# Tiles 10 to 13 of the second down projection as seven block products, and a reordered last norm

## The chip, the cores and the metric

The kernel runs on one core of one Trainium2 chip. The metric is the device time of one execution in microseconds (us), lower is better. A core has TensorE (PE, matmuls; PEld is its loading of the stationary operand), VectorE (DVE), ScalarE (ACT), GpSimd (POOL) and SyncE (SP, which here only issues DMAs). Each works through its own queue in order and waits for the others by semaphores. SBUF is the on-chip memory, PSUM holds the matmuls' sums in banks.

## The reference

A decoder trunk of two layers over 512 positions of 1024 channels. Each layer has a mixer and a gated feed-forward part (FFN) with a convolution of width 3 along the positions; a last RMS norm ends it. The change lies in layer 1's FFN and in the last norm:

```python
def gated_conv_ffn(x, w_gate, w_up, conv_w, conv_b, w_down):
    g = jnp.einsum('bsd,df->bsf', x, w_gate)
    g = causal_dwconv3(g, conv_w) + conv_b
    up = jnp.einsum('bsd,df->bsf', x, w_up)
    return jnp.einsum('bsf,fd->bsd', jax.nn.silu(g) * up, w_down)

hn = rms_norm(h, norm_ffn[layer])
h = h + gated_conv_ffn(hn, ...)
...
return rms_norm(h, final_norm)
```

All is float32. `D_FF` is 2816, that is 22 tiles of 128 hidden rows; the kernel calls such a tile `ft`, 0 to 21.

## The kernel before, in words

**Three matmuls for one.** A float32 operand is split into a high part, rounded to the type that TensorE takes at full rate (`F32R`), and a low part, the rest. Each product of two operands is three matmuls: high by high, high by low, low by high. ACT writes the high part (a copy). The low part is made in one of two ways. `parts` has DVE subtract the high part from the source. `summed` has ACT write the source with the sign turned into the low part's tile, and a DMA issued by POOL then accumulates the source onto it. That DMA waits for ACT's copy, and the tile may be used when it has landed.

**The steps of the FFN.** `Ffn.hidden(f)` makes the hidden tiles f and f+1 (f = 0, 2, ... 20; "step f"). From f = 2 on, gate (g) and up (u) are each multiplied by Strassen's scheme: seven block products in place of eight, so 14 per step, each of 12 matmuls of 128x256. The order is written out in `products`: g1, u1, g5, g6, u5, u6, g2, g7, u2, u7, g4, g3, u4, u3 (letter and number of the product). The weights and their sums (`s12`, `s34`) are made by `prepare(f)` on DVE and split into high and low parts. g's products 1, 6, 7 and 4 use one PSUM bank one after the other (`BANK`, "a"): ACT copies the bank to SBUF (`after`, L736), and only then may PE start the next product in it. DVE adds the other products onto these copies (L741, L746), then come the scaling by the norm's factor (L756), the convolution (L576), the silu on ACT (L584), and the multiplication with the up rows (L760 to L766). The results are the rows `s`, one 128x512 tile for each ft.

**The down projection of layer 1.** `split_acts` splits rows into high and low parts (L260, L262). `half_down(a, b, half)` multiplies the tiles a to b-1 with half of the 1024 output columns: for four tiles 4 x 4 x 3 = 48 matmuls of 128x512. DVE adds the four sums onto `y[t]` (L1104), t being one of four tiles of 128 positions. `STEPS` says which half follows which step: after step 6 the tiles 2 to 5 with half 0, after step 8 with half 1, and so on. So tiles 10 to 13 come after step 14 (half 0) and after step 16 (half 1), tiles 14 to 17 after 18 and 20.

**The last four tiles, 18 to 21.** They are multiplied by Strassen's scheme as well: the rows and the positions make a 2 by 2 block matrix, and so do the weights, `raw_dn18_00` to `_11` with four fetches. Seven products of 12 matmuls of 128x512 replace two halves of 48. `less` makes four sums of weights on DVE, the rows' sums are made on half rows of 128x256, `block` splits them into `hg` tiles (which are free then), and `put` splits the weights with `summed`. `product(p, i)` issues six matmuls for one block row i, `add` brings the sum into y. A product's sum goes to two places in Strassen's scheme; here it is folded into the operands so that each product's sum is added once per block row, 14 adds in all.

**The tail.** While those seven run, the last norm of each finished row begins. `taken` is an add into y, `squared` an ACT pass that sums squares, `halved` a 128x1 step on DVE, `rooted` ACT's square root, `inverted` three 128x1 steps on DVE, `times` the product of a row with the norm's gain, and `scaled` the multiplication with the row's factor, with the DMA that writes it out. `inorder` keeps the order in which these lines are written.

**What sets the order.** Outside the tail, a scheduler orders each engine's queue when the program is built. `behind(ins, first)` sets only an order, and in the down part `less` is placed behind `ffn.added["u"]`, the DVE add after u's product 7. Tiles share buffers by tag: four buffers for raw weights (`raw`), six each for high and low parts (`whi`, `wlo`), four each for the rows' high and low parts (`ahi`, `alo`), three for sums of weights (`sum`). A fetch into a raw buffer waits until the last reader of its former tile is done.

Of the kernel before, what the change touches and what calls it, by code (L numbers as in the profile page):

```python
# [15 lines left out]
P = 128  # L16
D = 1024
# [14 lines left out]
def tile_trunk(ctx: ExitStack, tc: tile.TileContext, x, norm_mix, norm_ffn, final_norm,  # L32
# [13 lines left out]
    def mm_bank(name):  # L46
        return ps_mm.tile([P, 512], F32, tag="mm", name=name)
# [505 lines left out]
    class Ffn:  # L553
# [10 lines left out]
        def __init__(self, layer, prm, norm, ap, sums):  # L564
            self.layer, self.prm, self.ap, self.acts = layer, prm, ap, {}
            self.norm, self.sums = norm, sums
# [13 lines left out]
        def silu(self, c, ft):  # L580
            name = f"s{self.layer}_{ft}"
            s = (self.ap.tile([P, S], F32, tag="s", bufs=3, name=name) if ft % 2 else
                 tp.tile([P, S], F32, tag="sq", name=name))
            nc.scalar.activation(s, c, AF.Silu, bias=self.prm("bf", ft))  # L584
            return s
# [493 lines left out]
    def ffn1(norm):  # L1079
        with tc.tile_pool(name="f1", bufs=1) as ap:  # L1080
# [4 lines left out]
            ffn = Ffn(1, prm1, norm, ap, sums)  # L1085
# [21 lines left out]
            def half_down(a, b, half):  # L1107
# [13 lines left out]

            a = NF - 4
            rows = {ft: row for ft, row in ffn.steps(half_down, before)}
            raw = {(i, j): fetch(
                w_ffn_down[1][(a + 2 * i) * P : (a + 2 * i + 2) * P, j * 512 : j * 512 + 512]
                .rearrange("(k p) c -> p k c", p=P), 2, 512, f"dn{a}_{i}{j}")
                for i, j in ((0, 0), (0, 1), (1, 1), (1, 0))}
            fin = ap.tile([P, D], F32, tag="sum", bufs=3, name="fin")  # L1130
            nc.scalar.dma_start(
                fin, final_norm.rearrange("(o d) -> o d", o=1).to_broadcast([P, D]))
            b11, b12, b21, b22 = (raw[at][0] for at in ((0, 0), (0, 1), (1, 0), (1, 1)))
            t1, t2 = (ap.tile([P, 2, S], F32, tag="sum", bufs=3, name=f"dnt{i}") for i in (1, 2))
            stat = {}

            def put(product, how, src):
                stat[product] = how(src, 2, 512, f"dnp{product}")

            def less(dst, x, y_):  # L1140
                behind(nc.vector.tensor_tensor(dst, x, y_, ALU.subtract), ffn.added["u"])

            less(t1, b12, b11)
            put(1, summed, b11)
            put(2, summed, b21)
            less(t2, b22, t1)
            put(5, summed, t1)
            put(6, summed, t2)
            less(b12, b22, b12)
            put(3, summed, b22)  # L1150
            put(7, summed, b12)
            less(b21, b21, t2)
            put(4, summed, b21)

            blocks = {}

            def block(product, n, srcs):
                hi, lo = (x.rearrange("p (a b) -> p a b", a=2) for x in hg[n])
                blocks[product] = hi, lo
                if not isinstance(srcs, list):  # L1160
                    nc.scalar.activation(hi, srcs, AF.Copy)
                    nc.vector.tensor_tensor(lo, srcs, hi.bitcast(F32), ALU.subtract)
                    return None
                for i, src in enumerate(srcs):
                    ins = nc.scalar.activation(hi[:, i], src, AF.Copy)
                    nc.vector.tensor_tensor(lo[:, i], src, hi[:, i].bitcast(F32), ALU.subtract)
                return ins

            a11, a12 = ([rows[a + 2 * i + n][:, :HALF] for n in range(2)] for i in range(2))
            a21, a22 = ([rows[a + 2 * i + n][:, HALF:] for n in range(2)] for i in range(2))  # L1170
            s1, s2 = (ap.tile([P, 2, HALF], F32, tag="c", bufs=2, name=f"dns{i}") for i in (1, 2))
            block(1, 0, a11)
            block(2, 1, a12)
            for n in range(2):
                nc.vector.tensor_tensor(s1[:, n], a21[n], a22[n], ALU.add)
            block(5, 4, s1)
            for n in range(2):
                nc.vector.tensor_tensor(s2[:, n], s1[:, n], a11[n], ALU.subtract)
            block(6, 5, s2)
            for n in range(2):  # L1180
                nc.vector.tensor_tensor(a12[n], a12[n], s2[:, n], ALU.subtract)
            last_split = block(3, 6, a12)
            for n in range(2):
                nc.vector.tensor_tensor(a21[n], a11[n], a21[n], ALU.subtract)
            block(7, 2, a21)
            block(4, 3, a22)
# [3 lines left out]
            banks = {}  # L1190

            def product(p, i, c0=0, c1=512, bank=None):

                at = bank or BANK[p], i
                first = at not in banks
                if first:
                    banks[at] = mm_bank(f"dn{a}_{at[0]}{i}")
                ps = banks[at][:, c0:c1]
                cs = slice(i * P, (i + 1) * P)
                (l_hi, l_lo), (r_hi, r_lo) = blocks[p], stat[p]  # L1200
                for k in range(2):
                    for l, r, end in ((l_hi, r_hi, False), (l_hi, r_lo, False),
                                      (l_lo, r_hi, k == 1)):
                        nc.tensor.matmul(ps, l[:, k, cs], r[:, k, c0:c1], start=first, stop=end,
                                         skip_group_check=True)
                        first = False
                return ps
# [5 lines left out]
            def taken(p, i, cs, bank=None):  # L1213

                t = i + 2 * (p in (5, 7, 4))
                part = cs if bank else slice(0, 512)
                inorder(add(y[t][:, cs], product(p, i, part.start, part.stop, bank), t))
# [6 lines left out]
            def halved(t, cs, first):  # L1224

                ss, ms = ssf[:, t, cs.start // 256 : cs.start // 256 + 1], ssf[:, t, 3:4]
                inorder(vec.tensor_scalar(ms, ss, -0.5 / D, -0.5 * EPS, op0=ALU.mult, op1=ALU.add)
                        if first else
                        vec.scalar_tensor_tensor(ms, ss, -0.5 / D, ms, op0=ALU.mult, op1=ALU.add))
# [4 lines left out]
            def inverted(t):  # L1234
                ms, r = ssf[:, t, 3:4], factor[t]
                inorder(vec.reciprocal(r, root[t]))
                inorder(vec.scalar_tensor_tensor(ms, ms, r, r, op0=ALU.mult, op1=ALU.mult))
                inorder(vec.scalar_tensor_tensor(r, ms, 1.5, r, op0=ALU.add, op1=ALU.mult))
# [35 lines left out]
            times(vec, 2, left)  # L1274
# [13 lines left out]
            squared(1, right)  # L1288
            halved(3, left, False)
            rooted(3)  # L1290

            first, second = slice(0, 256), slice(256, 512)
            taken(2, 1, first, "c")
            squared(1, first)
            halved(1, right, True)
            taken(2, 1, second, "d")
# [48 lines left out]
```

## Time and profile before

| | |
|---|---|
| time, median of 3 runs | 988.8 us (988.59 to 989.36) |
| the profiled execution | 988.85 us, its span 987.1 us |
| DVE busy | 775.9 us, 79% of the span |
| ACT busy | 562.0 us, 57% |
| POOL busy | 112.0 us, 11% |
| granted TensorE clock, mean | 0.998 |
| HBM | 102 GB/s over the span |

The span is what the profiler sees of the engines' work; the time holds 1.75 us more. In rows of the timeline the columns are the start and the length of an instruction in us, its engine, its line in the kernel, the operation, output <- inputs, and the shape; a bracket gives the idle time before it and what ended it. Matmuls are pipelined, so that the length of one (0.39 us) is more than the distance between two starts. A DVE or ACT row also is somewhat longer than the distance to the next start. Buffer numbers are left out of names: `raw_dn` stands for each weight tile of the down part. SPq and POOLq are the DMAs that these queues issue, with the time from the issue to the landing as the last number of a row in the view of issues.

### The profile page before, as it was taken

To read this page: it belongs to the slowest core of one execution; us is meant where nothing else is said; L and a number is where in the kernel's file an instruction comes from. 1 tells how busy PE (TensorE), PEld (TensorE's weight loads), DVE (VectorE), ACT (ScalarE), POOL (GpSimd) and SP (SyncE) were. 2 spreads that over 40 slices of the span, in tenths; PEclk is the share of its full clock that TensorE was granted. 3 is DMA by queue.
4 is the path that set the end of the run, shared out by engine and by line. 5 is a ranking of instruction groups with operands and counts; after the bars stand their busy time and mean duration, and the time that the engine had idled before them with its cause. 6 is when DMAs were issued, how large, how long until landed. Compare 5 with 4: busy or idle time off the path is not lost.

```text
span 987.1 us, 15485 instructions
## 1 busy us (share of the span) xinstructions
PE 975.2 (99%) x6099; PEld 879.9 (89%) x6099; DVE 775.9 (79%) x1181; ACT 562.0 (57%) x843; POOL 112.0 (11%) x129
## 2 busy tenths in 40 slices
PE   9999999999999999999999999999999999999996
PEld 6788888999999999999889988889999999999985
DVE  5797458998788887886887765589987779777787
ACT  5623347755465654655488734576655456554675
POOL 2142022000000000000210001210000000000022
PEclk9999999999999999999999999999999999999999
DMA  7442225555465454653324623264565465445573
GB/s 248 131 150 85 86 86 128 135 137 157 129 150 133 132 142 129 150 130 108 126 64 120 198 69 106 55 140 128 150 166 133 130 149 147 119 135 135 161 151 116
DMA packets 87942, 129.32 MB, mean 131 GB/s; under 512 B 4309, under 2 KB 57789, under 8 KB 87869
## 3 DMA queue, kind: packets, MB, share of 16 engines
q1 hardware_dynamic: 78172, 98.69, 32.2%
q0 software_dynamic: 8208, 27.79, 15.5%
q10 hardware_dynamic: 1488, 1.84, 0.6%
q8 instruction: 48, 0.79, 0.3%
q14 instruction: 26, 0.20, 0.1%
HBM read 98.42 MB, written 2.10 MB: 102 GB/s over the span
## 4 chain that ended last, share of the span: by engine, by line
PE 85%; DVE 8%; ACT 2%; issue 1%; DMA 0%; POOL 0%; ACTq 0%; DVEq 0%
PE dn L153 3%; PE dn L154 3%; PE dn L155 3%; PE d L153 3%; PE d L154 3%; PE d L155 3%; PE oo L155 1%; PE oo L153 1%; PE oo L154 1%; PE oe L154 1%; PE oe L153 1%; PE oe L155 1%; PE u_20a L542 1%; PE u_18a L542 1%; PE u_16a L542 1%
## 5 line engine op out<-in xcount | busy, mean ns | idle before, releaser
L576 DVE SCALAR_TENSOR_TENSOR c<-rows,prm,c 128x512 f32<-128x512 f32 x88 | 64.1, 747 | 1.5 <-ACT c L574 1.4
L140 POOL DMA_DIRECT2D wlo_g<-raw_g x20 | 17.2, 859 | 387.4 <-ACT wlo_g L139 350.4
L153 PE MATMUL d<-a_hi,whi_d 128*128 128x512 f32 x144 | 56.1, 390 | 0.0
L153 PE MATMUL dn<-whi_dn,a_hi 128*128 128x512 f32 x144 | 56.1, 390 | 0.0
L154 PE MATMUL dn<-wlo_dn,a_hi 128*128 128x512 f32 x144 | 56.1, 390 | 0.0
L154 PE MATMUL d<-a_lo,whi_d 128*128 128x512 f32 x144 | 56.1, 390 | 0.0
L155 PE MATMUL d<-a_hi,wlo_d 128*128 128x512 f32 x144 | 56.0, 389 | 0.0
L155 PE MATMUL dn<-whi_dn,a_lo 128*128 128x512 f32 x144 | 56.0, 389 | 0.0
L679 DVE TENSOR_TENSOR wlo_s34u<-s34u,whi_s34u 128x1024 fp32r<-128x1024 f32 x20 | 24.5, 1224 | 25.5 <-ACT whi_s34u L678 25.5
L149 DVE TENSOR_TENSOR wlo_dn<-raw_dn,whi_dn 128x1024 fp32r<-128x1024 f32 x18 | 22.0, 1225 | 23.6 <-ACT whi_dn L148 23.4
L142 ACT ACTIVATE whi_u<-raw_u 128x1024 fp32r<-128x1024 f32 x21 | 22.2, 1055 | 31.6 <-PE d L154 17.5
L149 DVE TENSOR_TENSOR wlo_d<-raw_d,whi_d 128x1024 fp32r<-128x1024 f32 x18 | 22.0, 1224 | 19.5 <-ACT whi_d L148 19.5
L198 ACT ACTIVATE hgh<-h,prm 128x512 fp32r<-128x512 f32 x24 | 17.3, 722 | 35.1 <-DVE h L309 35.0
L140 POOL DMA_DIRECT2D wlo_u<-raw_u x21 | 18.1, 860 | 162.0 <-ACT wlo_u L139 83.7
L584 ACT ACTIVATE s<-c,prm 128x512 f32<-128x512 f32 x44 | 31.2, 714 | 7.3 <-DVE c L576 7.2
L209 POOL TENSOR_TENSOR ssq_f<-ssq_f,sq_f 128x512 f32<-128x512 f32 x14 | 19.7, 1410 | 132.3 <-ACT sq_f L208 97.5
L260 ACT ACTIVATE a_hi<-s 128x512 fp32r<-128x512 f32 x40 | 25.0, 626 | 15.7 <-PE dn L154 9.9
L199 DVE SCALAR_TENSOR_TENSOR hgl<-h,prm,hgh 128x512 fp32r<-128x512 f32 x24 | 23.2, 965 | 12.0 <-ACT hgh L198 11.9
L155 PEld LDWEIGHTS d<-a_hi,wlo_d 128*128 128x128 f32 x144 | 27.0, 188 | 5.7
L155 PEld LDWEIGHTS dn<-whi_dn,a_lo 128*128 128x128 f32 x144 | 27.0, 188 | 5.7
L1104 DVE SCALAR_TENSOR_TENSOR y<-dn,small,y 128x512 f32<-128x512 f32 x40 | 27.7, 748 | 5.5 <-PE dn L155 5.5
L153 PEld LDWEIGHTS d<-a_hi,whi_d 128*128 128x128 f32 x144 | 27.1, 188 | 5.3
(1489 smaller groups left out, 3762.7 us busy)
## 6 DMA issues: line engine op xcount, KB each, us to landing
raw_g<-in_w_ffn_gate_dram SPq DMA_DIRECT2D x40, 512.0 KB, 3.8
raw_u<-in_w_ffn_up_dram SPq DMA_DIRECT2D x40, 512.0 KB, 3.7
raw_dn<-in_w_ffn_down_dram SPq DMA_DIRECT2D x22, 512.0 KB, 3.6
wlo_u<-raw_u POOLq DMA_DIRECT2D x21, 512.0 KB, 5.7
wlo_g<-raw_g POOLq DMA_DIRECT2D x20, 512.0 KB, 4.6
raw_d<-in_w_ffn_down_dram SPq DMA_DIRECT2D x18, 512.0 KB, 3.7
raw_oe<-in_w_out_even_dram SPq DMA_DIRECT2D x8, 512.0 KB, 3.6
raw_v<-in_w_in_odd_dram SPq DMA_DIRECT2D x8, 512.0 KB, 4.5
```

The lines of the kernel that those rows point to most:

```text
L140: nc.gpsimd.dma_start(lo, raw, accum_op=ALU.add)
L149: behind(nc.vector.tensor_tensor(lo, raw, hi.bitcast(F32), ALU.subtract), after[0])
L153: nc.tensor.matmul(ps, lhs[0], rhs[0], start=start, stop=False)
L154: nc.tensor.matmul(ps, lhs[0], rhs[1], start=False, stop=False)
L155: nc.tensor.matmul(ps, lhs[1], rhs[0], start=False, stop=stop)
L199: nc.vector.scalar_tensor_tensor(hg[k][1], h[k], g, hg[k][0].bitcast(F32), op0=ALU.mult, op1=ALU.subtract)
L260: nc.scalar.activation(hi, src, AF.Copy, scale=scale)
L542: nc.tensor.matmul(ps, l, r, start=first, stop=end, skip_group_check=True)
L576: nc.vector.scalar_tensor_tensor(c, t[:, i : S + i], prm("cf", i * NF + ft), c, op0=ALU.mult, op1=ALU.add)
L584: nc.scalar.activation(s, c, AF.Silu, bias=self.prm("bf", ft))
L679: nc.vector.tensor_tensor(lo, src, hi.bitcast(F32), ALU.subtract)
L1104: return nc.vector.scalar_tensor_tensor(dst, ps, ffn.cols[:, t : t + 1], dst, op0=ALU.mult, op1=ALU.add)
```

## The change

The code of the last four tiles becomes a class `Seven`, which can be used for any four tiles, and it is used for tiles 10 to 13 too (`sevens = (10,)`). The main loop of layer 1's FFN is written out in `ffn1` instead of in `steps`. After step 12 `part.acts` splits the rows of tiles 10 to 13 and makes their sums; the rows stay whole for that, and the silu of tile 14 writes into a tile with the tag `ssq`. After step 14 `part.weights` fetches and splits the weights (products 3, 7 and 4 by DVE, the other four with accumulating DMAs), and `part.run` issues the seven products. After step 16 no down part follows. In the tail, 128x1 steps on DVE become `tensor_scalar` with the second operand as a scalar per partition, three of the products with the gain move from DVE to GpSimd, two scalings move to DVE and two of row 1's squares become one.

```diff
+            if ft in self.apart:
+                s = tp.tile([P, S], F32, tag="ssq", bufs=1, name=name)
...
+            class Seven:
...
+                def block(self, product, srcs, home=None):
+                    name = f"dnb{self.a}_{product}"
+                    hi, lo = home or (ap.tile([P, S], F32R, tag=f"a{x}", bufs=4,
+                                              name=f"{name}_{x}") for x in ("hi", "lo"))
...
+                def acts(self, rows, home={}):
+                    a = self.a
+                    a11, a12 = ([rows[a + 2 * i + n][:, :HALF] for n in range(2)]
+                                for i in range(2))
+                    a21, a22 = ([rows[a + 2 * i + n][:, HALF:] for n in range(2)]
+                                for i in range(2))
+                    s1, s2 = (ap.tile([P, 2, HALF], F32, tag="c", bufs=2, name=f"dns{a}_{i}")
+                              for i in (1, 2))
+                    self.block(1, a11, home.get(1))
+                    self.block(2, a12, home.get(2))
+                    for n in range(2):
+                        nc.vector.tensor_tensor(s1[:, n], a21[n], a22[n], ALU.add)
+                    self.block(5, s1, home.get(5))
...
+                def weights(self, between, by_vector=()):
...
+                    def put(product, src):
+                        how = parts if product in by_vector else summed
+                        self.stat[product] = how(src, 2, 512, f"dnp{a}_{product}")
+
+                    def less(dst, x, y_):
+                        behind(nc.vector.tensor_tensor(dst, x, y_, ALU.subtract),
+                               ffn.added["u"])
+
+                    less(t1, b12, b11)
+                    put(1, b11)
+                    put(2, b21)
+                    less(t2, b22, t1)
+                    put(5, t1)
+                    put(6, t2)
+                    less(b12, b22, b12)
+                    put(3, b22)
+                    put(7, b12)
+                    less(b21, b21, t2)
+                    put(4, b21)
...
+                def run(self):
+                    for p in (1, 2, 5, 6, 3, 7, 4):
+                        for i in range(2):
+                            t = i + 2 * (p in (5, 7, 4))
+                            cs = left if p in (1, 2, 4) else right
+                            add(y[t][:, cs], self.product(p, i), t)
+                        if p in (1, 2, 5):
+                            self.block(*self.rest.pop(0))
...
+            part = None
+            for f in range(0, NF, 2):
+                multiplied(f)
+                a = f - 4
+                if part:
+                    part.weights(lambda: None, (3, 7, 4))
+                    part.run()
...
+                    split_rows(f + 1, f)
...
+                if f > 0 and f % 4 == 0 and f - 2 in sevens:
+                    part = Seven(f - 2)
+                    part.acts(rows)
...
-                inorder(vec.tensor_scalar(ms, ss, -0.5 / D, -0.5 * EPS, op0=ALU.mult, op1=ALU.add)
-                        if first else
-                        vec.scalar_tensor_tensor(ms, ss, -0.5 / D, ms, op0=ALU.mult, op1=ALU.add))
+                inorder(vec.tensor_scalar(ms, ss, -0.5 / D, -0.5 * EPS if first else ms,
+                                          op0=ALU.mult, op1=ALU.add))
...
-                inorder(vec.scalar_tensor_tensor(ms, ms, r, r, op0=ALU.mult, op1=ALU.mult))
-                inorder(vec.scalar_tensor_tensor(r, ms, 1.5, r, op0=ALU.add, op1=ALU.mult))
+                inorder(vec.tensor_scalar(ms, ms, r, r, op0=ALU.mult, op1=ALU.mult))
+                inorder(vec.tensor_scalar(r, ms, 1.5, r, op0=ALU.add, op1=ALU.mult))
...
-            times(vec, 2, left)
+            times(pool, 2, left)
...
+            times(pool, 3, right)
...
-            scaled(act, 2, left)
-            scaled(pool, 2, right)
+            scaled(act, 2, right)
...
-            times(vec, 3, right)
+            scaled(vec, 2, left)
...
-            squared(1, right)
+            times(pool, 1, right)
...
+            scaled(vec, 3, left)
+            scaled(pool, 3, right)
```

In the built order of the changed kernel, PE has 12 matmuls fewer, DVE 24 instructions more, ACT 13 and POOL 4 more. DVE makes the sums of step 16's weights behind the last add of the seven, and PE starts the first four matmuls with the high parts of step 16 within the seven.

More of the change, by code (lines that the diff above doesn't have):

```diff
@@ L553, in tile_trunk, with __init__ @@
     class Ffn:
-        def __init__(self, layer, prm, norm, ap, sums):
+        def __init__(self, layer, prm, norm, ap, sums, apart=()):
             self.layer, self.prm, self.ap, self.acts = layer, prm, ap, {}
+            self.apart = apart
             self.norm, self.sums = norm, sums
@@ L1083, in sums @@
                         for k in (kp, kp + NP)]
-            ffn = Ffn(1, prm1, norm, ap, sums)
+            sevens = (10,)
+            ffn = Ffn(1, prm1, norm, ap, sums, [a + 4 for a in sevens])
             acts = ffn.acts
@@ L1120, in half_down @@
                       lambda t, ps: add(y[t][:, cs], ps, t))
[L1124 to L1129, printed above, removed]
-            fin = ap.tile([P, D], F32, tag="sum", bufs=3, name="fin")
@@ L1131, in ffn1 @@
[L1131 to L1178, printed above, removed]
@@ L1188, in ffn1, with fetch_fin @@
+            last = Seven(NF - 4)
+            fin = ap.tile([P, D], F32, tag="sum", bufs=3, name="fin")
+            def fetch_fin():
+                nc.scalar.dma_start(
+                    fin, final_norm.rearrange("(o d) -> o d", o=1).to_broadcast([P, D]))
+            last.weights(fetch_fin)
+            homes = dict(zip((1, 2, 7, 4, 5, 6, 3), hg))
+            last.acts(rows, homes)
+            last_split = [last.block(*x) for x in last.rest][0]
             first_root = work("sd", 1, "first")
@@ L1189, in ffn1 @@
             behind(nc.scalar.activation(first_root, eps, AF.Sqrt), last_split)
[L1190 to L1207, printed above, removed]
@@ L1216, in taken @@
                 part = cs if bank else slice(0, 512)
-                inorder(add(y[t][:, cs], product(p, i, part.start, part.stop, bank), t))
+                inorder(add(y[t][:, cs], last.product(p, i, part.start, part.stop, bank), t))
             def squared(t, cs):
```

100 lines of the change are left out of this document (79 added, 21 removed).

## The prediction

> **What bounds the kernel now.** First the totals and the chain of waits on the page of before, then the stages one by one.
>
> ```profile
> PE 975.2 (99%) x6099; PEld 879.9 (89%) x6099; DVE 775.9 (79%) x1181; ACT 562.0 (57%) x843; POOL 112.0 (11%) x129
> PE 85%; DVE 8%; ACT 2%; issue 1%; DMA 0%; POOL 0%; ACTq 0%; DVEq 0%
> ```
>
> TensorE (PE) sets the end nearly everywhere. So a removed matmul shortens the run, as long as the other engines still deliver in time. Whether they do is a question of the stretch that changes. The view of busy time by stretch gives, for step 14 with its down half, step 16 with its down half, and that down half alone:
>
> ```profile
> 833.98:865.04 31.06, 31.06 (x217) 29.16 (x216) 24.22 (x37) 16.43 (x24) 1.72 (x2) 1.00 0.53 141
> 865.04:896.10 31.06, 31.06 (x217) 29.17 (x216) 24.68 (x39) 17.63 (x27) 1.72 (x2) 1.00 0.51 132
> 854.13:865.04 10.91, 10.91 (x50) 9.02 (x49) 9.22 (x15) 5.58 (x7) 1.72 (x2) 1.00 0.74 190
> ```
>
> The columns are the length, then busy time of PE, its weight loads, VectorE (DVE), ScalarE (ACT), GpSimd (POOL), the granted clock (1.00), DMA share and GB/s. PE has no gap. DVE is busy 24.22 + 24.68 = 48.9 us of 62.1, which leaves 13.2 us over two steps. Step 14 holds 14 products before its down half, 20.15 / 14 = 1.44 us each.
>
> **The saving on PE.** Two down halves for tiles 10 to 13 go (2 x 48 matmuls of 128x512) and seven products of 12 such matmuls come. The last seven of before show what one product costs:
>
> ```profile
> 958.22 0.39 PE L1204 MATMUL dn_a<-whi_dnp,hgh 128*128 128x512 f32 x1
> 960.94 0.39 PE L1204 MATMUL dn_b<-whi_dnp,hgh 128*128 128x512 f32 x1
> ```
>
> Twelve matmuls lie between these starts: 2.72 us. Seven are 19.04 us against 2 x 10.91 = 21.82. The gain is 2.75 us, the middle between that difference and 12 matmuls at 2.72 / 12.
>
> **The price on DVE.** The spacing of starts, not the busy time, counts for a queue that never rests:
>
> ```profile
> 856.69 0.42 DVE L760 TENSOR_TENSOR s<-kept,s 128x256 f32<-128x256 f32 x1
> 857.02 0.42 DVE L761 TENSOR_TENSOR s<-u_14a,s 128x256 f32<-128x256 f32 x1
> 857.36 1.22 DVE L679 TENSOR_TENSOR wlo_s12g<-s12g,whi_s12g 128x1024 fp32r<-128x1024 f32 x1
> 858.49 0.69 DVE L766 TENSOR_TENSOR s<-kept,s 128x512 f32<-128x512 f32 x1
> 859.09 1.22 DVE L679 TENSOR_TENSOR wlo_s34g<-s34g,whi_s34g 128x1024 fp32r<-128x1024 f32 x1
> ...
> 863.20 2.79 DVE L1104 SCALAR_TENSOR_TENSOR y<-dn,small,y 128x512 f32<-128x512 f32 x4 [1.69 <-PE dn L155]
> ```
>
> That is 0.335 for 128x256, 1.13 for 128x1024, 0.60 for 128x512 and about 0.66 for an add into y (2.79 for four). Added: 4 `less` (4.52), 3 low parts of weights (3.39), 8 sums of half rows (2.68), low parts of row blocks (10 x 0.335 + 2 x 0.60 = 4.55), 14 adds into y (9.24): 24.4 us. Removed: 4 low parts of weights (4.52), 4 of rows (2.40), 8 adds (5.28): 12.2 us. The net 12.2 us would nearly fill the 13.2, while the two steps shrink by 2.75. It fits only if evenly spread, and it isn't: `less` of t1 is ordered behind the u add of product 7 in step 14, so most of it comes after that.
>
> **Step 14: a fetch that ScalarE waits for.** In the changed order ACT takes the two copies of `raw_dn10_10` (for product 2) ahead of its copy of g's product 7, and PE's next product in that bank, g's product 4, waits for that copy. Before, these came at their own time:
>
> ```profile
> 845.70 0.37 ACT L736 COPY rows<-g_14a 128x256 f32<-128x256 f32 x1 [1.63 <-PE g_14a L542]
> 848.58 0.37 ACT L736 COPY kept<-u_14a 128x256 f32<-128x256 f32 x1 [2.51 <-PE u_14a L542]
> 848.37 0.40 PE L542 MATMUL g_14a<-t,whi_g 128*128 128x256 f32 x2
> ```
>
> So g's copy has 2.4 us to spare. The fetch takes the raw buffer of step 14's second u weights, and must wait for the DMA that accumulates their low part. That one was issued before step 14 began; now its first ACT copy stands behind the copy of g's product 1:
>
> ```profile
> 829.05 1.05 ACT L139 ACTIVATE wlo_u<-raw_u 128x1024 fp32r<-128x1024 f32 x1
> 830.40 0.86 POOL L140 DMA_DIRECT2D wlo_u<-raw_u  x1 [6.34 <-ACT wlo_u L139]
> 831.08 0.37 SPq L129 DMA_DIRECT2D raw_g<-in_w_ffn_gate_dram  x1
> 835.62 0.37 ACT L736 COPY rows<-g_14a 128x256 f32<-128x256 f32 x1
> raw_dn<-in_w_ffn_down_dram SPq DMA_DIRECT2D x22, 512.0 KB, 3.6
> wlo_g<-raw_g POOLq DMA_DIRECT2D x20, 512.0 KB, 4.6
> wlo_u<-raw_u POOLq DMA_DIRECT2D x1, 512.0 KB, 5.6
> raw_g<-in_w_ffn_gate_dram SPq DMA_DIRECT2D x1, 512.0 KB, 6.1
> ...
> wlo_u<-raw_u POOLq DMA_DIRECT2D x1, 512.0 KB, 7.2
> ```
>
> (The last three rows are the view of DMA issues for two short windows: two rows of 831.0 to 831.2, and the accumulate issued at 860.9 together with a fetch.) The copy runs 835.9 to 836.9, the DMA is issued 0.3 later at 837.2, as after 829.05, and lands 4.6 to 5.6 later, 841.8 to 842.8. The fetch is issued then, beside the accumulate of product 1's low part, which I place at 842.4 (its copy stands behind whi_s34u, which now waits for DVE until 839.9, and one copy). A fetch issued 0.7 us from an accumulate took 6.1 us, one alone 3.6. From 842.1 it lands at 848.2, or at 845.7 if it runs alone. I take 6.1, since the pair is the same. Two ACT copies (0.96 each by spacing) and the 0.26 of g's copy end at 850.4: **PE stalls 2.05 us** at g's product 4. With 3.6 they end at 847.9, and the stall is nothing.
>
> **The seven.** The third DVE add behind that copy ends at 851.5, and then t1 starts. From there to the last add into y the changed order has 42 DVE instructions in a row: 7 of 128x1024 (7.9 us), 4 steps of the convolution and 14 adds into y at 0.66 (11.9), 7 of 128x512 (4.2), 10 of 128x256 (3.35). That is 27.3 us, ending at 878.8. PE, from 850.4, does four products of step 14 (5.75) and would reach the end of the seven at 856.2 + 19.04 = 875.2, or 875.7 with four matmuls of step 16 that the order puts between them. But product 3 needs the bank that the adds of product 5 free, the first of them DVE's 27th instruction, 18.3 us into its run, at 869.8, and PE would be there at 867.6. The seven end at 878.0: **2.25 us**. DVE's queue itself is the bound here, so nothing covers it.
>
> **Step 16's weights.** Before, DVE had the sums for the next step about 10 us early:
>
> ```profile
> 877.50 0.68 DVE L698 TENSOR_TENSOR s12g<-raw_g,raw_g 128x512 f32<-128x512 f32 x1
> 882.39 1.06 ACT L678 ACTIVATE whi_s12g<-s12g 128x1024 fp32r<-128x1024 f32 x1
> ```
>
> (These are for step 18; it began at 896.1.) Now s12g of step 16 stands behind the last add. Its two passes with one of s34g between end at 880.7, ACT's copy at 881.7, the pass for its low part at 883.0. PE finishes g1 and u1 at 880.4 and needs it for g5: **2.6 us**; u5's low part comes 0.3 late too. The other 12 products bring step 18 to 883.3 + 17.3 = 900.6, where before it began at 896.1. The four raw buffers, held by dn10 until its low parts are done, delay step 16's fetches; by my walk they land before DVE asks. The accumulate for u's product 2 is issued at 885.8 by the same walk and due at 891.9: with 5.6 it is in time, with 7.2 it is 1.1 late, and one more ACT copy ahead of it makes 1.4. I take 0. Steps 18 and 20 have the 79% load again, so the shift of 4.45 (2.05 + 2.25 + 2.6 + 0.3 - 2.75) stays to the tail. No bound goes below a gain of 2.75.
>
> **The tail.** There DVE sets the end, and 128x1 steps with two tensors wait for a GpSimd product:
>
> ```profile
> 970.17 1.29 POOL L1241 TENSOR_TENSOR yf<-y,fin 128x512 f32<-128x512 f32 x1 [7.03 <-DVE ssf L1229]
> 976.94 1.27 POOL L1241 TENSOR_TENSOR yf<-y,fin 128x512 f32<-128x512 f32 x1
> 970.62 0.85 DVE L1237 SCALAR_TENSOR_TENSOR ssf<-ssf 128x1 f32<-128x1 f32 x1
> 974.76 0.22 DVE L1237 SCALAR_TENSOR_TENSOR ssf<-ssf 128x1 f32<-128x1 f32 x1
> 975.76 0.14 DVE L1227 TENSOR_SCALAR ssf<-ssf 128x1 f32<-128x1 f32 x1
> 977.20 1.03 DVE L1229 SCALAR_TENSOR_TENSOR ssf<-ssf 128x1 f32<-128x1 f32 x1
> 981.68 0.75 DVE L1307 SCALAR_TENSOR_TENSOR y<-y,ssf,fin 128x512 f32<-128x512 f32 x1
> ```
>
> 0.85 and 1.03 end with the product (971.46, 978.21); undisturbed it is 0.22. The tensor_scalar form has one tensor and should be free of this: 0.6 + 0.8. Also three products of 0.60 leave DVE, and two scalings of 128x512 come. PE's last matmul ends near 977.5 in any case, so not all counts. Walking the new order with these spacings, the last multiply starts at 979.9 to 980.4 instead of 981.68; I take **1.5 us**, between 0 (scaling blocked by GpSimd) and 1.7.
>
> The Trainium skill (SBUF — State Buffer, "Who interferes with whom") states this lock for two SBUF inputs, and the two rows agree. It goes on against the change: a tensor_scalar from SBUF to SBUF can run in a mode that uses both ports, and then it too waits for a whole GpSimd instruction. No row here has a 128x512 one beside GpSimd.
>
> **Sum.** The profiled run took 988.85 (its span is 987.1, 1.75 around it), as good as the median, 988.8. 988.85 + 4.45 - 1.5 = 991.8 us.
>
> **Rivals.**
> - *The fetch lands in time* (3.6 us). Only the stall in step 14 goes: 991.8 - 2.05 = 989.8. For it: the median of the page. Against: 831.08.
> - *The saving is kept*: DVE is never late, because fetches land early and the low parts spread into its 13.2 us. 988.85 - 2.75 - 1.5 = 984.6, faster. For it: PE led in every step. Against: 27.3 us in one run while PE needs 24.8 for the same stretch. It would need t1 to start by 847, but product 7 of u, behind which t1 is ordered, ends at 848.4; the chance is for a wait that I misplaced.
> - *Tensor_scalar waits as well*: the scaling of row 3 stands behind two GpSimd instructions (1.3 + 1.8 us), and the last multiply comes 0.6 later than before: 991.8 + 2.1 = 993.9.
> - *Step 16 is later still*: the accumulate for u's product 2 takes the 7.2 us that one issued with a fetch took: 991.8 + 1.4 = 993.2. For it: three of step 16's fetches start late.
> - That the change does not do what it says is out: the built order has 12 matmuls fewer.
>
> **How the numbers follow.** Changes within 0.2% (1.98 us, 986.8 to 990.8) can't be told from none. Forecast 0.52, fetch in time 0.16, saving kept 0.14, tensor_scalar blocked 0.06, later still 0.07, parts of the stalls only (near 990) 0.05. Faster: 0.14. Same: 0.16 + 0.05 and 0.03 of the forecast's lower edge, 0.24. Slower: 0.62. The forecast's own range is 990.5 to 993. The range goes down to the case with the fetch in time, with 1 us for the terms, 988.6, and up to the last two rivals, 994.2; the saving kept is left out.
>
> **What would show it.** Right: PE idle about 2 us before g's product 4 of step 14, with the two copies of raw_dn ahead of ACT's copy; DVE without idle time from t1 to the last add of the seven; PE waiting in front of product 3 and of g5 in step 16; 128x1 steps of 0.15 to 0.22 beside GpSimd. Wrong: step 18 starting before 897, DVE idle inside the seven, or a tensor_scalar as long as the GpSimd product beside it.

## The result, and the profile after

The changed kernel took 993.91 us, the median of five runs (991.53 to 996.26), against 988.80 for the kernel before (five runs, 988.54 to 989.96): a ratio of 1.0048, with a 95% interval of 1.0037 to 1.0059. It is slower by 0.5%. The five runs lie 4.7 us apart, those of before 1.4. One of the 11 runs of g3 below took 1373 us at a granted clock of 0.65, where the other ten took 988 to 990, and its ratio is that of the ten.

The profiled execution took 994.67 us with a span of 992.0; the one before took 988.85 with 987.1. Its busy time by engine, and the shares of its chain of waits:

```profile
PE 974.1 (98%) x6087; PEld 877.6 (88%) x6087; DVE 785.4 (79%) x1204; ACT 569.7 (57%) x855; POOL 117.7 (12%) x135
PE 74%; DVE 12%; issue 4%; DMA 3%; ACT 3%; POOL 0%; ACTq 0%; POOLq 0%; SPq 0%; DVEq 0%
```

Twelve matmuls are gone. PE carries 74% of the chain instead of 85%; what it lost went to DVE, DMA, ACT and "issue". DVE's share of the span is 79%, the same as before, so the average says nothing about where it got stuck. The view of busy time by stretch does: step 14, the seven products, step 16, step 18, and the tail of the changed kernel (columns as in the prediction).

```profile
834.07:855.14 21.07, 20.40 (x169) 20.19 (x168) 13.14 (x20) 13.21 (x20) 3.44 (x4) 1.00 0.68 155
855.14:877.11 21.97, 20.24 (x91) 16.30 (x90) 21.95 (x35) 10.92 (x18) 1.72 (x2) 1.00 0.58 136
877.11:899.90 22.79, 20.43 (x165) 19.81 (x164) 18.12 (x27) 14.38 (x20) 1.72 (x2) 1.00 0.72 189
899.90:922.22 22.32, 20.68 (x171) 20.28 (x169) 19.94 (x33) 14.90 (x24) 1.72 (x2) 1.00 0.44 118
964.19:992.00 27.81, 19.57 (x91) 15.95 (x89) 21.57 (x53) 15.22 (x33) 10.15 (x8) 0.92 0.47 125
```

The same view of before, for step 18 and the tail:

```profile
896.10:916.25 20.15, 20.15 (x169) 20.14 (x168) 15.00 (x23) 10.85 (x18) 0.00 (x0) 1.00 0.41 113
958.22:987.05 28.83, 19.57 (x91) 15.95 (x89) 23.09 (x54) 16.09 (x36) 7.66 (x6) 0.92 0.45 121
```

A step alone is 20.15 us. Step 14 has 0.92 on top. One product of the seven takes 2.75 us here (dn_a starts at 855.14, dn_b at 857.89), 19.25 for seven, and four matmuls of step 16 stand between them (0.5 us): 21.97 - 19.25 - 0.5 leaves 2.2 of waiting, and DVE is busy for 21.95 of the 21.97. Step 16, without those four, has 22.79 + 0.5 - 20.15 = 3.1 too many, and step 18, where the prediction expected nothing, 2.17. From the end of step 18 to the tail it is 41.97 us in both kernels (922.22 to 964.19; 916.25 to 958.22). So PE reaches the tail 5.97 us late.

The waits themselves, in the timeline of the changed kernel; a bracket names what ended the idle time. First step 14, ACT and then PE:

```profile
846.97 1.06 ACT L139 ACTIVATE wlo_dnp<-raw_dn 128x1024 fp32r<-128x1024 f32 x1 [3.70 <-DMA raw_dn<-in_w_ffn_down_dram]
847.94 1.04 ACT L142 ACTIVATE whi_dnp<-raw_dn 128x1024 fp32r<-128x1024 f32 x1
848.88 0.35 ACT L740 COPY rows<-g_14a 128x256 f32<-128x256 f32 x1
849.29 0.51 PE L542 MATMUL g_14a<-t,whi_g 128*128 128x256 f32 x2 [0.67 <-ACT rows L740]
```

ACT sat idle for 3.70 us before a fetch that its next instruction needed, while the bank of g's product 7 stood ready behind it. The copy came at 848.88 instead of 845.70, and PE's next product 0.83 late (848.37 for that product's first row before, 848.46 with this run's step starting 0.09 later).

Then the seven, with the last adds into y, and step 16:

```profile
850.27 1.22 DVE L1193 TENSOR_TENSOR dnt<-raw_dn,raw_dn 128x1024 f32<-128x1024 f32 x1
...
863.79 0.47 PE L1220 MATMUL dn_a<-whi_dnp,dnb_hi 128*128 128x512 f32 x1 [0.30 <-DVE y L1110]
...
868.81 0.50 PE L1220 MATMUL dn_e<-whi_dnp,dnb_hi 128*128 128x512 f32 x1 [1.43 <-DVE y L1110]
...
877.97 0.68 DVE L702 TENSOR_TENSOR s12g<-raw_g,raw_g 128x512 f32<-128x512 f32 x1
...
881.08 0.50 PE L542 MATMUL g_16e<-t,whi_s12g 128*128 128x256 f32 x2 [1.42 <-ACT whi_s12g L682]
882.34 0.39 PE L542 MATMUL g_16e<-t,wlo_s12g 128*128 128x256 f32 x1 [0.52 <-DVE wlo_s12g L683]
...
891.41 0.39 PE L542 MATMUL u_16b<-hgh,wlo_u 128*128 128x256 f32 x1 [0.42 <-DMA wlo_u<-raw_u]
```

From t1 (850.27) to the first instruction after the last add (877.97), DVE worked 27.7 us without a pause. PE waited twice for sums to leave their banks, and then for the weights of step 16 that stood behind the last add.

Last step 18, POOL's and SP's DMA issues and then DVE, ACT and PE:

```profile
890.48 0.86 POOL L140 DMA_DIRECT2D wlo_g<-raw_g  x1 [4.33 <-ACT wlo_g L139]
891.50 0.37 SPq L129 DMA_DIRECT2D raw_u<-in_w_ffn_up_dram  x1
...
897.62 0.69 DVE L702 TENSOR_TENSOR s12u<-raw_u,raw_u 128x512 f32<-128x512 f32 x1 [2.45 <-DMA raw_u<-in_w_ffn_up_dram]
...
906.63 1.04 ACT L682 ACTIVATE whi_s12u<-s12u 128x1024 fp32r<-128x1024 f32 x1
907.72 0.51 PE L542 MATMUL u_18e<-t,whi_s12u 128*128 128x256 f32 x2 [1.50 <-ACT whi_s12u L682]
```

The weights for step 18 were fetched 1.0 us after an accumulating DMA had been issued, and took 6.1 us. DVE stood idle for 2.45 us, and the copy that u's product 5 needs came 1.5 us too late.

### The profile page after: what moved, and what is told of

It reads as the page before. It is cut to its first block, busy times and chain, and to the rows that moved or that the text cites. A ratio compares the mean times of both kernels' runs of the same rounds, so it can differ in the third digit from the quotient of the medians.

```text
span 992.0 us, 15508 instructions
## 1 busy us (share of the span) xinstructions
PE 974.1 (98%) x6087; PEld 877.6 (88%) x6087; DVE 785.4 (79%) x1204; ACT 569.7 (57%) x855; POOL 117.7 (12%) x135
## 4 chain that ended last, share of the span: by engine, by line
PE 74%; DVE 12%; issue 4%; DMA 3%; ACT 3%; POOL 0%; ACTq 0%; POOLq 0%; SPq 0%; DVEq 0%
PE d L153 3%; PE d L155 3%; PE d L154 3%; PE dn L154 2%; PE dn L153 2%; PE dn L155 2%; PE oo L155 1%; PE oo L154 1%; PE oo L153 1%; PE oe L155 1%; PE oe L154 1%; PE oe L153 1%; DVE y L1110 1%; PE g_20a L542 1%; PE u_12a L542 1%
## 5 line engine op out<-in xcount | busy, mean ns | idle before, releaser
L153 PE MATMUL dn<-whi_dn,a_hi 128*128 128x512 f32 x112 | 43.7, 390 | 0.0
L154 PE MATMUL dn<-wlo_dn,a_hi 128*128 128x512 f32 x112 | 43.7, 390 | 0.0
L155 PE MATMUL dn<-whi_dn,a_lo 128*128 128x512 f32 x112 | 43.6, 389 | 0.0
L575 ACT ACTIVATE c<-rows,prm 128x512 f32<-128x512 f32 x44 | 31.1, 710 | 4.1 <-DVE rows L760 4.1
L154 PEld LDWEIGHTS d<-a_lo,whi_d 128*128 128x128 f32 x144 | 27.1, 188 | 5.3
L260 ACT ACTIVATE a_hi<-s 128x512 fp32r<-128x512 f32 x36 | 22.5, 625 | 13.8 <-PE dn_e L1220 4.4
L148 ACT ACTIVATE whi_d<-raw_d 128x1024 fp32r<-128x1024 f32 x18 | 19.0, 1058 | 19.3 <-issue 11.1
```

The source lines that it names most:

```text
L153: nc.tensor.matmul(ps, lhs[0], rhs[0], start=start, stop=False)
L154: nc.tensor.matmul(ps, lhs[0], rhs[1], start=False, stop=False)
L155: nc.tensor.matmul(ps, lhs[1], rhs[0], start=False, stop=stop)
L260: nc.scalar.activation(hi, src, AF.Copy, scale=scale)
L575: nc.scalar.activation(c, t[:, 0:S], AF.Copy, scale=prm("cf", ft))
```

## The experiments

Each group ran on one chip, together with the kernel before: e1 to e4 beside 988.78, f1 to f3 beside 989.13, g1 to g3 beside 988.81, h1 and h2 beside 988.89. A ratio is to that one.

**Which half of the change loses.** e1 is the changed kernel with the old down part (`sevens = (10,)` becomes `()`); e2 keeps the seven and has the old tail.

> The new tail with the old down part (no tiles in blocks but the last four). My theory, that the loss lies in steps 14 to 18 and the tail is a gain of about 1 us: 987.3 to 988.2, steps 14 to 20 as before, PE without a gap there. Rival, that the new tail costs (its 128x1 tensor_scalar steps took 0.27 where scalar_tensor_tensor took 0.22 undisturbed): 989 or more.

> The seven products for tiles 10 to 13 with the old tail. My theory: the loss is all here, about 1 us more than the full change, 994 to 996; the tail's 128x1 steps beside GpSimd products take 0.8 to 1 us again. Rival, that the tail is to blame: about 989 to 990.

e1: 987.78 us (11 runs), ratio 0.9990 (0.9982 to 0.9999). e2: 995.40 (5 runs), 1.0078 (1.0064 to 1.0091). The tail is a gain of 1.0 us, the seven a loss of 6.6; their sum is 5.6, and both together lost 5.1. In e2 the stall of step 14 was larger:

```profile
851.28 0.51 PE L542 MATMUL g_14a<-t,whi_g 128*128 128x256 f32 x2 [2.69 <-ACT rows L740]
```

PE came there 2.0 us later than in the changed kernel's own profile, with the same order of fetches.

**The late fetch.** The four weight blocks are fetched in an order in which the one for product 2 no longer waits for a buffer.

```diff
-for i, j in ((0, 0), (0, 1), (1, 1), (1, 0)):
+for i, j in (((0, 0), (1, 0), (0, 1), (1, 1)) if a == 10 else ((0, 0), (0, 1), (1, 1), (1, 0))):
```

> The full change, with the fetch for product 2 of tiles 10 to 13 second instead of last. My theory: the fetch lands before step 14 needs ScalarE, the stall at g's product 4 (0.8 us in the trace of the change) goes, and what comes behind it starts that much earlier: 992.5 to 993.5, with less spread between runs, since the landing of that fetch no longer counts. Rival, that the fetch is the root of all stalls behind: 989 or less.

992.61 us (991.64 to 992.90, 5 runs), 1.0039 (1.0025 to 1.0052). The stall of step 14 is gone (g's product 4 starts at 848.50), and the runs lie within 1.3 us instead of 4.7, so that this fetch is a likely source of the spread; it is not the only one, as f2, f3 and g1 below, with the early fetch too, spread over 2.7 to 3.2 us in 11 runs. Step 18 nevertheless began at 899.86, as late as in the changed kernel. The rows of e3 around step 16's first wait, and the stretch that holds them:

```profile
878.53 0.28 PE L542 MATMUL u_16a<-hgh,wlo_a 128*128 128x256 f32 x1
880.23 0.50 PE L542 MATMUL g_16e<-t,whi_s12g 128*128 128x256 f32 x2 [1.42 <-ACT whi_s12g L682]
...
882.93 0.41 PE L542 MATMUL g_16e<-t,wlo_s12g 128*128 128x256 f32 x1
883.15 0.63 PE L542 MATMUL g_16e<-t,whi_s12g 128*128 128x256 f32 x2
883.57 0.41 PE L542 MATMUL g_16e<-t,wlo_s12g 128*128 128x256 f32 x1
```

The view of stretches of e3, for the 11 us around it:

```profile
879.00:890.00 11.00, 9.26 (x62) 9.05 (x63) 8.36 (x12) 9.25 (x13) 0.86 (x1) 0.84 0.74 193
```

After a pause of 1.70 us the same matmuls stand 0.21 us apart instead of 0.12, and the granted clock of the stretch is 0.84. In this execution that took back what the fetch order had given. Step 18, on the other hand, took 20.22 us: its u weights were fetched 0.4 us ahead of the accumulating DMA instead of 1.0 behind it, and DVE had them by 895.36.

**DVE's work in the run.** Two experiments take work from DVE's run. In e4 all seven weights get their low parts by accumulating DMAs (`part.weights(lambda: None, ())`), which takes three passes of 1.13 us away and adds three DMAs. g1, on top of e3, takes the same passes away and adds nothing: products 3, 7 and 4 use the low part of product 6 in place of their own.

```diff
-how = parts if product in by_vector else summed
-self.stat[product] = how(src, 2, 512, f"dnp{a}_{product}")
+if product in by_vector:
+    hi = wp.tile([P, 2, 512], F32R, tag="whi", bufs=6, name=f"whi_dnp{a}_{product}")
+    nc.scalar.activation(hi, src, AF.Copy)
+    self.stat[product] = hi, self.stat[6][1]
+    return
+self.stat[product] = summed(src, 2, 512, f"dnp{a}_{product}")
```

> The full change, with the low parts of products 3, 7 and 4 made by ScalarE and an accumulating DMA instead of DVE. It takes 3 x 1.13 = 3.4 us out of DVE's unbroken run and adds three transfers. My theory, that DVE's queue is the bound: the seven and step 16's weights come 2 to 3.4 us earlier, 990.5 to 992. Rival, that transfers set the pace (late fetches and accumulates): the raw buffers stay taken until the accumulates have landed, and it is slower than the change, 995 or more.

> The variant with the early fetch, without the three passes of DVE that make the low parts of products 3, 7 and 4: these products use product 6's low part in their place, so part of the computation is changed. PE has the same matmuls, no transfer is added, and DVE's queue is the same but for these 3 x 1.13 = 3.4 us. My theory, DVE's unbroken run as the bound: the seven's stalls (2 us) go, the last add and all behind it come 2.7 us earlier: 989.5 to 990.5. Rival, that transfers set the pace: no change, 992 or more.

e4: 995.84 us (992.80 to 997.01, 5 runs), 1.0064 (1.0050 to 1.0077). That missed my forecast and met the time of the rival, but its rows don't show the rival's reason. ACT and PE in e4:

```profile
849.31 1.06 ACT L139 ACTIVATE wlo_dnp<-raw_dn 128x1024 fp32r<-128x1024 f32 x1 [5.74 <-DMA raw_dn<-in_w_ffn_down_dram]
...
851.63 0.50 PE L542 MATMUL g_14a<-t,whi_g 128*128 128x256 f32 x2 [2.70 <-ACT rows L740]
...
874.29 0.63 ACT L682 ACTIVATE whi_a<-raw_u 128x512 fp32r<-128x512 f32 x1 [5.17 <-DMA raw_u<-in_w_ffn_up_dram]
```

The late fetch of product 2's block landed 2.3 us later than in the changed kernel's profile. In e2, which has none of the added DMAs, it landed as late (848.97), so that this is not shown to be their doing. From the start of step 14 to that of step 18 e4 took 67.7 us and e2 67.5, and part of e4's time went to a granted clock of 0.84 that e2 doesn't have (last section). What the added DMAs did delay is a fetch for step 16: it was issued at 866.87 instead of 860.78, when an accumulating DMA had read its raw buffer, and ACT waited 5.17 us for it. The seven themselves took 20.8 us instead of 22.0. So the three DMAs brought no gain; whether they cost more than the three passes stays open.

g1: 989.78 us (11 runs), 1.0011 (1.0002 to 1.0020), 2.8 less than e3 for 3.4 us of passes. The stretch of g1 in which the seven run:

```profile
854.00:873.00 19.00, 19.00 (x87) 15.74 (x86) 18.69 (x32) 11.07 (x19) 1.72 (x2) 1.00 0.64 157
```

And its waits of PE after them:

```profile
877.06 0.50 PE L542 MATMUL g_16e<-t,whi_s12g 128*128 128x256 f32 x2 [0.87 <-ACT whi_s12g L682]
878.32 0.39 PE L542 MATMUL g_16e<-t,wlo_s12g 128*128 128x256 f32 x1 [0.52 <-DVE wlo_s12g L683]
...
903.61 0.51 PE L542 MATMUL u_18e<-t,whi_s12u 128*128 128x256 f32 x2 [1.50 <-ACT whi_s12u L682]
```

PE has no gap in the seven any more: they take their 19 us. So the length of DVE's run was what held them. The waits in step 16 (shorter) and step 18 remain, and eat the saving.

**Moving DVE's work out of the stretch.** f1 is e3 with three of the four sums of weights no longer ordered behind the u add. f3 is e3 with the split of two tiles' rows moved behind step 16. f2 has both.

```diff
-       ffn.added["u"])
+       ffn.added["u"] if a > 10 or dst is b21 else None)
```
```diff
-split_rows(f + 1, f)
...
-split_rows(f + 1, f)
+split_rows(f - 1, f - 2, f + 1, f)
```

> The variant with the early fetch, and t1, t2 and the third difference of weights no longer ordered behind u's product 7, so that DVE makes them (3 x 1.13 = 3.4 us) in its idle time in step 14. My theory, DVE's unbroken run as the bound: that run is 2 to 3.4 us shorter, the seven's stalls of 2 us nearly go, step 16's weights stay late behind the last add: 990 to 991.3. Rival, that transfers and buffers set the pace here too: as the variant with the early fetch, 992 to 993.

> As the variant with the early sums, and the low parts of rows 14 and 15, which no product needs before step 18 is over, made after step 16: 1.2 us less on DVE within the seven, and in the built order the sums of s12g come ahead of the last adds. My theory: the stall before g5 of step 16 goes (2.5 us) as well, the saving of 2.7 us shows: 985.5 to 988. Rival, that step 16 waits for its fetches or its accumulates, whose buffers the seven hold: 989.5 or more.

> The variant with the early fetch and the late rows 14 and 15, with the sums of weights where the change has them. My theory: the seven's run is 1.2 us shorter and s12g comes ahead of the last adds, about 2 us less than the variant with the early fetch: 990 to 991.5, above the one with both. Rival, as above: 992 to 993.

f1: 992.67 us (5 runs), 1.0039 (1.0026 to 1.0051), no gain over e3. The sums now stand where their data is late; DVE in f1:

```profile
843.75 1.23 DVE L1194 TENSOR_TENSOR dnt<-raw_dn,raw_dn 128x1024 f32<-128x1024 f32 x1 [1.72 <-DMA raw_dn<-in_w_ffn_down_dram]
...
846.84 1.23 DVE L1194 TENSOR_TENSOR dnt<-raw_dn,dnt 128x1024 f32<-128x1024 f32 x1 [1.86 <-DMA raw_dn<-in_w_ffn_down_dram]
...
851.87 1.23 DVE L1194 TENSOR_TENSOR raw_dn<-raw_dn,dnt 128x1024 f32<-128x1024 f32 x1 [1.34 <-DMA wlo_dnp<-raw_dn]
```

The first two waits fall in time in which DVE is idle in e3 too. The third is the one that counts: the fourth sum overwrites a tile that the accumulating DMA of product 2 reads, so it began at 851.87, and the first instruction after the last add came at 876.98, hardly earlier than e3's 877.12. The seven took 21.8 us, in e3 22.0. Step 18 began 1.6 us before e3's, which had lost most of that to the clock, but it took 22.43 us instead of 20.22: its u weights were again fetched behind an accumulating DMA, by 0.5 us. f3: 989.84 us (11 runs), 1.0007 (0.9998 to 1.0016), 2.8 less than e3 and just below the range that I gave. f2: 989.55 us (11 runs), 1.0003 (0.9994 to 1.0012), above what I expected (985.5 to 988). In f3 the waits inside the seven stand as before; step 16's are short, since its weights come ahead of that work; the stretch of step 16:

```profile
875.50:897.00 21.50, 21.04 (x168) 20.43 (x167) 20.95 (x32) 15.97 (x23) 1.72 (x2) 1.00 0.76 181
```

DVE is busy in 20.95 of these 21.50 us. Even so no version with the seven has a median below that of the kernel before; f2 and f3 can't be told from it.

**Another place.** g2 does the same for tiles 6 to 9 (`sevens = (6,)`).

> The full change with tiles 6 to 9 in place of 10 to 13, so that the seven products run behind step 10. My theory: the built order is the same there, DVE's run too, so the loss is the same: 992 to 996. Rival, that step 14's place (where the fetches of the last steps come close) is to blame: 988 or less.

996.49 us (4 runs), 1.0078 (1.0063 to 1.0094), slightly above the range. The loss doesn't come from the neighbours of tiles 10 to 13.

**The tail's two halves.** g3 is the kernel before with only the 128x1 steps as `tensor_scalar`; h2 is the same again, for its profile. h1 is e1 with those steps as they were.

> The kernel before with nothing changed but the 128x1 steps of the last norm: tensor_scalar with a scalar per partition in place of scalar_tensor_tensor. My theory: they no longer wait for GpSimd's product (0.6 and 0.8 us less), PE's end hides part of it, and this is most of the new tail's gain of 1.0 us: 987.8 to 988.3. Rival, that the moved products give the gain: 988.6 to 989.

> The new tail with the old down part, but with scalar_tensor_tensor kept for the 128x1 steps, so that only the placing of the products and scalings differs from before. With five products on GpSimd, the steps meet them more often. If either part alone is enough: 987.8 to 988.2 here. If the two need each other (the run with the steps alone showed no gain): 988.6 or more, with 128x1 steps of 0.8 to 1.3 us beside GpSimd's products.

> The kernel before with tensor_scalar steps again, for a profile. If the steps did wait for GpSimd and no longer do, they take 0.15 to 0.3 us here beside GpSimd's products, and the last multiply starts where it did, at 981.3 to 981.8, because PE's last products or ScalarE's squares end last. If tensor_scalar waits as well, 0.8 to 1 us.

g3: 988.66 us, 0.9999 (0.9990 to 1.0008); h1: 989.24 us, 1.0002 (0.9993 to 1.0011), 11 runs each; h2's one run took 988.46. Neither half alone gives anything that can be told from nothing, and I had expected some from g3. A step beside GpSimd's product in h1, with the old form:

```profile
975.03 1.30 POOL L1317 TENSOR_TENSOR yf<-y,fin 128x512 f32<-128x512 f32 x1 [0.76 <-DVE ssf L1312]
975.06 1.28 DVE L1313 SCALAR_TENSOR_TENSOR ssf<-ssf 128x1 f32<-128x1 f32 x1
```

And in h2, with the new one:

```profile
976.85 1.27 POOL L1240 TENSOR_TENSOR yf<-y,fin 128x512 f32<-128x512 f32 x1
977.11 0.20 DVE L1227 TENSOR_SCALAR ssf<-ssf 128x1 f32<-128x1 f32 x1
```

The old form waits for the product's end, the new one doesn't. With the new form alone DVE still has its own products, and little is won (h2's last multiply starts at 981.28, before at 981.68); with the products moved to GpSimd and the old form, DVE waits for each of them. Together they take 1.0 us.

## Why the prediction was right

The forecast, 991.8 us in a range of 988.6 to 994.2 and slower, held: the median is 2.1 above it. The mechanism is the one it named, but for step 18. The sizes, from the two profiled executions:

| step of the prediction | predicted | measured |
|---|---|---|
| PE's saving | -2.75 | -2.6 (21.82 - 7 x 2.75) |
| step 14 waits for a copy behind a late fetch | +2.05 | +0.92; in e2 and e4 2.9 |
| the seven, bound by DVE's run of 27.3 us | +2.25 | +2.2; the run is 27.7 |
| step 16's weights behind the last add | +2.9 | +3.1, of it 0.6 another wait |
| step 18 starts late by | 4.45 | 3.80 |
| step 18 and after | 0 | 2.17 on PE, 0.8 more on DVE |
| tail | -1.5 | -1.2 |

*Step 14.* ACT did take the two copies ahead of g's. The fetch landed at 847.0, between the 845.7 of the rival and the 848.2 of the forecast, so that the profile shows less than half of the stall. e2 and e4, with this order, were 2.9 late (851.28 in e2, where 848.43 is due). So the size was off in both directions, by when the fetch came in. e3 gave the rival "the fetch lands in time" its condition and took 992.6 us, not its 989.8: with this stall gone, DVE's run, step 16 and the clock after its pause keep the rest.

*The seven.* DVE without a pause, PE waiting at product 3: as forecast. The prediction put all of the wait at product 3; 0.45 us of it came at product 6. g1 shows that the length of DVE's run is the cause: with the three passes gone the waits are gone.

*Step 16.* g5 waited as forecast, 2.3 us instead of 2.6 (at 881.08 and 882.34, counted from start to start). The accumulate for u's product 2, taken as in time, cost 0.6 (at 891.41): it took 6.1 us instead of 5.6.

*The step that failed* is this one: "Steps 18 and 20 have the 79% load again, so the shift of 4.45 (2.05 + 2.25 + 2.6 + 0.3 - 2.75) stays to the tail." Step 18 lost 2.17 more. That load is an average too, and says nothing of when a transfer lands. The fetch for its u weights came right behind an accumulating DMA and took 6.1 us, the price that the prediction had used in step 14 for the same pair. g1 has this wait too, with a fetch 0.9 us behind; e3, with the fetch ahead of the accumulate, has a step 18 of 20.22 (all eight traces are compared in the last section). Beside it DVE lags too. The last sum of weights before the tail, in the kernel before, below the accumulating DMA for product 2 of the last seven:

```profile
947.33 0.86 POOL L140 DMA_DIRECT2D wlo_dnp<-raw_dn  x1 [1.65 <-DVE c L576]
...
952.21 1.22 DVE L1141 TENSOR_TENSOR raw_dn<-raw_dn,dnt 128x1024 f32<-128x1024 f32 x1 [1.03 <-issue]
```

And in the changed kernel:

```profile
953.29 0.86 POOL L140 DMA_DIRECT2D wlo_dnp<-raw_dn  x1 [1.65 <-DVE c L577]
...
959.00 1.23 DVE L1193 TENSOR_TENSOR raw_dn<-raw_dn,dnt 128x1024 f32<-128x1024 f32 x1 [1.86 <-issue]
```

It is 6.79 us later, 0.8 more than PE. The rows don't name what it waits for, but the sum overwrites the tile which that DMA reads. By the view of DMA issues the DMA took 4.8 us before (947.33 to 952.1) and 5.6 in the changed kernel (953.29 to 958.9), and both times the sum starts 0.1 after that; in f1 the same sum of tiles 10 to 13 names such a DMA. So the 0.8 is the longer time of this transfer. Why it took longer stays open.

*The tail.* From that row to the last multiply it was 29.47 us (to 981.68) and is 28.25 (to 987.25): 1.2 us won, of 1.5 forecast. e1 gives 1.0 by its median. One part of the rest is visible in the changed kernel, as is what became of the rival "tensor_scalar waits as well":

```profile
980.20 0.21 DVE L1303 TENSOR_SCALAR ssf<-ssf 128x1 f32<-128x1 f32 x1 [0.79 <-ACT sqf L1297]
...
981.15 1.30 POOL L1316 TENSOR_TENSOR yf<-y,fin 128x512 f32<-128x512 f32 x1 [0.37 <-DVE ssf L1311]
...
982.34 0.48 DVE L1321 TENSOR_SCALAR y<-yf,ssf 128x512 f32<-128x512 f32 x1
982.44 1.53 POOL L1316 TENSOR_TENSOR yf<-y,fin 128x512 f32<-128x512 f32 x1
...
983.92 1.27 POOL L1316 TENSOR_TENSOR yf<-y,fin 128x512 f32<-128x512 f32 x1
...
987.25 0.75 DVE L1379 SCALAR_TENSOR_TENSOR y<-y,ssf,fin 128x512 f32<-128x512 f32 x1
```

DVE, relieved, now waits 0.79 us for ACT's squares, a wait that took the place of the removed one. The scaling of 128x512 took 0.48 us, but that doesn't refute the rival. It began only 0.11 before the first of three GpSimd products ended, and the second product took 1.53 where its neighbours took 1.30 and 1.27. In h1 a scaling began 0.16 into GpSimd's own scaling, which took 1.57 (980.44 to 982.01):

```profile
980.60 0.81 DVE L1322 TENSOR_SCALAR y<-yf,ssf 128x512 f32<-128x512 f32 x1
```

So the two do hold each other up, in these rows by 0.2 to 0.3 us. How long a scaling would wait that starts early in a GpSimd product, no run here shows. The Trainium skill (SBUF — State Buffer, "Who interferes with whom") lets a tensor_scalar in a 2-port mode wait for a whole GpSimd instruction; the one in h1 ended 0.6 before GpSimd's did. The rival's time, 993.9, is the measured median by chance: it asked for a tail 0.6 slower than before, and the tail is 1.2 faster.

*The sum.* DVE's 6.8 at the tail, less 1.2, puts the last multiply 5.57 later (987.25 - 981.68); another 0.25 lies behind it. That is 5.82, the difference of the two executions (994.67 - 988.85). That the median lies in the range is in part luck: errors of opposite signs meet in it, 1.1 too much at step 14, 3.0 too little for step 18 and what follows and 0.3 too much gain for the tail. The profiled execution (994.67) and one other run (996.26) lie above the range, and with the late landing of e2 and e4 step 14 alone would have cost 1.9 more. The rival "the saving is kept" asked for t1 by 847. In f1 t1 did start at 843.75, and the seven still took 21.8 us, because the last sum of weights waited for a transfer. "Step 16 is later still", 993.2, comes near in size, but not in place: its transfer took 6.1 us and cost 0.6 in step 16, and the larger loss sat in step 18.

The version that beats both kernels is e1, the new tail with the old down part: 987.78 us, 0.1% below before and 0.6% below the changed kernel.

## What to carry to other kernels

A removed matmul is worth its time only where the engines that feed and empty PE have room in that very stretch: add up, by the spacing of starts, what an in-order queue must do between two points, and compare that with what PE needs between them. A share of busy time over the step, or over the span, hides it twice, in the stretch itself and in the steps after it that inherit late transfers. And before work is moved from an engine to DMAs, or earlier in a queue, look at when its data lands: here both moves met a second bound, the transfers, close behind the first.

## What the runs showed of the hardware that I had not expected

*The clock after short pauses.* In e3 a pause of 1.70 us (1.42 of it idle time) was followed by matmuls 0.21 us apart instead of 0.12, and the granted clock over 11 us was 0.84. The same pause in step 16 of the changed kernel left it at 1.00. Two pauses of one length differ as well. The 11 us of e2 behind its idle time of 2.69 us:

```profile
851.00:862.00 11.00, 10.72 (x70) 9.88 (x71) 10.74 (x18) 9.36 (x15) 1.91 (x3) 1.00 0.92 190
```

And of e4 behind 2.70:

```profile
851.00:862.00 11.00, 10.37 (x62) 9.85 (x63) 9.22 (x16) 8.67 (x14) 2.65 (x4) 0.84 0.89 183
```

The Trainium skill (TensorE: Matmul & The Clock Gate, "HAM oscillation — how this bites in real kernels") puts the pause that costs the clock above some 3.4 us; here shorter ones did it in some runs and not in others. What decides stays open.

*A fetch behind an accumulating DMA.* Eight traces have the seven at tiles 10 to 13. In five (the changed kernel, e2, e4, f1, g1) the fetch of step 18's u weights was issued 0.5 to 1.0 us after an accumulate; DVE had the weights 6.1 to 6.5 us later, PE waited 1.50 us at u's product 5, and step 18 took 22.3 to 22.5 us. In three (e3, f2, f3) it was issued 0.4 to 2.3 us before the accumulate, DVE had the weights within 5.0, and step 18 took 20.2. f2 and f3 also move work of DVE, and no run changes the order of these two issues alone, so that its part in the 2 us rests on this comparison.
